# A hybrid decoder step on one core: the delta net's substitution held in a PSUM bank, and two of its state products put ahead of ScalarE's read

## The chip, the core and the metric

The kernel runs on one core of a Trainium2 chip. Five engines work side by side, each through its own queue in the order in which its instructions stand: TensorE (PE, matmuls; PEld is its weight load), VectorE (DVE), ScalarE (ACT), GpSimd (POOL) and SyncE (SP, here only an issuer of DMAs; ACT issues DMAs too, written ACTq). The metric is device time in microseconds (us) of one execution; lower is better.

## The reference

One layer of a decoder trunk over a prompt of 1024 tokens and a sample batch of 8. A combined input projection feeds three groups of heads: differential attention (the sample rows attend to 4096 cached positions each, read as pages through a page table), a Mamba-2 state-space branch, and a gated delta net. Their outputs are joined and projected back. The part that is changed is the delta net, in chunks:

```
lower = where(strict, beta * kk * decay, 0)
sol   = triangular_solve(lower + eye, rhs, lower=True, unit_diagonal=True)
u, w  = sol[..., :DV_C], sol[..., DV_C:]
def step(S, inp):
    v_new = u_c - w_c @ S
    o     = qg_c @ S + attn_c @ v_new
    S     = S * gl_c + kd_c.T @ v_new
```

## The kernel before

The program is written as Python generators, one for each stream of work, that are advanced in turn (`drive`) by weights; the recorded instructions are then put in an order by a list scheduler, which fixes each engine's queue. Three stretches follow one another. In the front, to about 875 us, the projection (`proj_fm`, line 458: each product in three matmuls of split operands) shares the engines with the pages of the sample attention, with the delta net's heads 0, 1, 2 and with smaller streams. In the middle, to about 1172 us, come the prompt's attention, the state-space scan and head 3 of the delta net. The end is the output projection (line 1831).

The pages: SP loads two pages into a tile `kt` (three buffers); GpSimd multiplies it by the queries (line 840, both operands in SBUF); VectorE sums it (line 841) into `lg`. After 16 such pairs `page_softmax` (VectorE steps on `lg`, `smx`, TensorE at lines 851, 856 and 868) makes the weights with which TensorE multiplies the values, `pv` at line 896.

A head of the delta net (`gdn_head`): the decay-weighted products go to `LT` and `AT`; the diagonal 32x32 blocks go through DRAM (`invd`) and come back as `Dm`, with four blocks of a partition's own in a row. Then 31 steps of forward substitution run on VectorE, two instructions each: `tv` = column j of the unknowns `U` times row j of `Dm`, and `U` minus `tv`. `U` is an SBUF tile of 16x32 per partition: its first half holds the unknowns, which start as an identity that GpSimd copies there (line 1138), its second half is the scratch `tv`. In the trace both are called U, so a step reads as `U<-U,Dm` and `U<-U`, at line 159 where the helper `tt` records. `gstep` remembers the newest step, and a page's multiply is ordered behind it (`behind_gdn`). After the last step ACT issues the DMAs that write U to `invd` (line 1149) and read it back into `LT`; the larger blocks are then solved by small matmuls, and `u`, `w` are formed.

The recurrence follows, eight chunks one after the other. In a chunk all four products share one PSUM bank `ps`: w by the state and the queries by the state (lines 1218, 1219), then, once VectorE has made `vn`, the state's update and the output's second part (lines 1223, 1224). ScalarE reads the queries' product into `oC` (line 155, helper `act`), VectorE makes the new state `St` and adds the second part to `oC`.

PSUM has eight banks. One is `pv`. In the front the rest are two rings: `pj` with three for the projection, and `pm` with four for everything else; `ada_gate` holds one of the four over 32 matmuls (line 1013). The first items of the projection (`LEAD` = 5) are summed side by side in two `pj` and three `pm` banks. In the middle there are other rings (`PSB`), none of which changes.

Of the kernel before, what the change touches and what calls it, by code (L numbers as in the profile page):

```python
# [9 lines left out]
F32 = mybir.dt.float32  # L10
# [3 lines left out]
AF = mybir.ActivationFunctionType  # L14
# [33 lines left out]
WB = 3  # L48
RA, RT, RB, RS, RO = "ps", "pt", "pj", "pj", "pj"
PSB = {"pj": 3, "ps": 2, "pt": 1, "pd": 1}  # L50
PSA = {"pj": 3, "pm": 4}
RG = "pj"
RW = "pd"
RD = "pd"
# [24 lines left out]
def bl(ap, n):  # L79
    return ap.unsqueeze(len(ap.shape)).broadcast_to(list(ap.shape) + [n])  # L80


def bm(ap, n):
    return ap.unsqueeze(1).broadcast_to([ap.shape[0], n] + list(ap.shape[1:]))
# [3 lines left out]
def trunk_kernel(  # L88
# [56 lines left out]
    def bank(ring=None):  # L145

        r = ring or rings[-1]
        return PS[r].tile([P, 512], F32, tag="b", name=nm("b"))
# [9 lines left out]
    def tt(out, a, b, op):  # L158
        return V.tensor_tensor(out=out, in0=a, in1=b, op=op)  # L159
# [264 lines left out]
    def proj_fm(items, ws):  # L424

        def cols(n, halo):
            h0 = halo if n else 0
            N = CH + h0 + (h0 & 1)
            return N, h0, slice((n + 1) * CH - N, (n + 1) * CH)

        ps = [bank("pj" if i < 2 else "pm") for i in range(LEAD)]
        for k in range(8):
            for i in range(LEAD):
                N, h0, sl = cols(i % 3, items[i // 3][2])
                hi, lo = ws[i // 3][k]
                for e, (a, b) in enumerate(((hi, hh), (hi, hl), (lo, hh))):
                    TE.matmul(ps[i][:, 0:N], a, b[k][:, sl], start=(k == 0 and e == 0), stop=(k == 7 and e == 2))
            if k % 2 and k < 7:
                yield 3.5 * LEAD / 4
        for i in range(LEAD):  # L440
            N, h0, sl = cols(i % 3, items[i // 3][2])
            items[i // 3][1](i % 3, ps[i][:, N - CH - h0:N])
        yield 3.5 * LEAD / 4
        ps = ws[:-1] = []
        w = ws.pop()
        for j, (c0, sink, halo) in enumerate(items):
            if 3 * j + 2 < LEAD:
                continue
            raw = w_load(items[j + 1][0], SP if j < LQ else S) if j + 1 < len(items) else []
            wn = []  # L450
            for n in range(LEAD % 3 if j == LEAD // 3 else 0, 3):
                ps = bank("pj")
                N, h0, sl = cols(n, halo)
                i = 0
                for k in range(8):
                    hi, lo = w[k]
                    for a, b in ((hi, hh), (hi, hl), (lo, hh)):
                        TE.matmul(ps[:, 0:N], a, b[k][:, sl], start=(i == 0), stop=(i == 23))  # L458
                        i += 1
                sink(n, ps[:, N - CH - h0:N])  # L460
                if n == 2:
                    for r in raw[len(wn) // 4:]:
                        wn += w_split(r)
                elif raw:
                    wn += w_split(raw[n])
                yield 3.5
            w = wn
# [572 lines left out]
    def gdn_head(h):  # L1040
# [94 lines left out]
        T64 = half([96, 8, 64], n="T64")  # L1135
        with tc.issue_after(ld.ins):
            G.memset(T64[0:32, :, 32:64], 0.0)
        G.tensor_copy(out=U[:, 0:8], in_=eye8)
        gstep.clear()
        yield W1  # L1140
        for j in range(31):
            n, m = 31 - j, j // 4 + 1
            tv = U[:, 8:16].rearrange("p a b -> p (a b)")[:, 0:m * n].rearrange("p (c i) -> p c i", i=n)
            tt(tv, bl(U[:, 0:m, j], n), bm(Dm[:, j, j + 1:32], m), ALU.mult)
            step = tt(U[:, 0:m, j + 1:32], U[:, 0:m, j + 1:32], tv, ALU.subtract)
            gstep[:] = [step.ins]
            yield 0.5
        for g in range(4):
            S.dma_start(out=invd[1, h].rearrange("b c (i g) l -> (b c) g i l", g=4)[:, g], in_=U[32 * g:32 * g + 32, 0:8])
        for b in range(4):  # L1150
# [62 lines left out]
        for c in range(8):  # L1213
            cs = slice(c * P, (c + 1) * P)
            ps = bank()
            vn = u[:, 0, :]
            if c > 0:
                TE.matmul(ps[:, 0:P], w[:, c, :], St, start=True, stop=True)
                TE.matmul(ps[:, P:256], qT[:, cs], St, start=True, stop=True)
                vn = small([P, P], "vn")  # L1220
                tt(vn, u[:, c, :], ps[:, 0:P], ALU.add)
                act(o[:, c, :], ps[:, P:256], AF.Copy, scale=f1[:, c:c + 1])
            TE.matmul(ps[:, 256:384], kN[:, c, :], vn, start=True, stop=True)
            TE.matmul(ps[:, 384:512], AT[:, c, :], vn, start=True, stop=True)
            Sn = small([P, P], "St")
            if c > 0:
                stt(Sn, St, egt[:, c, 12 + h:13 + h], ps[:, 256:384], ALU.mult, ALU.add)
                tt(o[:, c, :], o[:, c, :], ps[:, 384:512], ALU.add)
            else:
                V.tensor_copy(Sn, ps[:, 256:384])  # L1230
                S.copy(o[:, c, :], ps[:, 384:512])
            St = Sn
            yield 5.0
# [708 lines left out]
```

## Time and profile before

| | before |
|---|---|
| median of 3 runs | 1307.45 us (1305.61 to 1309.79) |
| the profiled execution | 1311.91 us, its span 1310.2 us |
| PE busy | 1145.3 us, 87% of the span |
| DVE busy | 865.4 us, 66% |
| POOL busy | 583.9 us, 45% |
| ACT busy | 470.2 us, 36% |
| HBM | 209 GB/s over the span |
| mean granted TensorE clock | 0.945 |

The span runs from the first to the last instruction. Busy time is a mean over stretches with different limits; which wait ends last has to be read in each. An engine's row shows the idle time just before it in brackets, and what ended it. [...]

### The profile page before, as it was taken

To read this page: it belongs to the slowest core of one execution; us is meant where nothing else is said; L and a number is where in the kernel's file an instruction comes from. 1 tells how busy PE (TensorE), PEld (TensorE's weight loads), DVE (VectorE), ACT (ScalarE), POOL (GpSimd) and SP (SyncE) were. 2 spreads that over 40 slices of the span, in tenths; PEclk is the share of its full clock that TensorE was granted. 3 is DMA by queue.
4 is the path that set the end of the run, shared out by engine and by line. 5 is a ranking of instruction groups with operands and counts; after the bars stand their busy time and mean duration, and the time that the engine had idled before them with its cause. 6 is when DMAs were issued, how large, how long until landed. Compare 5 with 4: busy or idle time off the path is not lost.

```text
span 1310.2 us, 21966 instructions
## 1 busy us (share of the span) xinstructions
PE 1145.3 (87%) x7364; PEld 957.1 (73%) x7365; DVE 865.4 (66%) x1994; ACT 470.2 (36%) x997; POOL 583.9 (45%) x395
## 2 busy tenths in 40 slices
PE   4999989988899678979886889888988999799997
PEld 3789987767688458759765778865656868688876
DVE  5623695398577749745656947678867888674444
ACT  6332232212213322222352142416626767552111
POOL 3757864453464634454645558453013142251100
PEclk9999999998899889989998889997889999899999
DMA  8657866984785863775779499799678473871410
GB/s 293 190 184 235 269 197 201 287 272 129 276 276 183 274 193 110 239 255 169 258 265 260 147 292 328 205 285 278 179 234 214 117 197 100 291 236 49 145 67 34
DMA packets 246449, 275.55 MB, mean 210 GB/s; under 512 B 31905, under 2 KB 163376, under 8 KB 246322
## 3 DMA queue, kind: packets, MB, share of 16 engines
q1 hardware_dynamic: 168082, 214.44, 50.9%
q10 hardware_dynamic: 78256, 59.72, 16.1%
q8 instruction: 58, 0.95, 0.3%
q14 instruction: 53, 0.43, 0.1%
HBM read 231.59 MB, written 42.67 MB: 209 GB/s over the span
## 4 chain that ended last, share of the span: by engine, by line
PE 40%; DVE 23%; DMA 19%; issue 5%; ACT 5%; POOL 4%; SPq 3%; ACTq 1%; POOLq 0%; DVEq 0%
PE b L458 15%; PE b L1831 9%; DVE U L159 5%; DMA kt<-in_cache_k_dram 4%; PE pv L896 3%; DVE cy L167 3%; DVE lg L841 3%; POOL kt L840 2%; DMA w<-in_w_in_dram 2%; DMA vt<-in_cache_v_dram 2%; DMA gs<-in_state_gdn_dram 1%; PE b L745 1%; DVE cy L969 1%; DVE e L721 1%; DMA Dm<-invd 1%
## 5 line engine op out<-in xcount | busy, mean ns | idle before, releaser
L458 PE MATMUL b<-hh,whi 128*128 128x344 f32 (+1 forms) x2016 | 505.5, 333 | 29.5 <-DVE cy L167 23.3
L840 POOL TENSOR_TENSOR kt<-kt,qb 128x1024 f32<-128x1024 f32 x128 | 305.9, 2395 | 258.4 <-DMA kt<-in_cache_k_dram 185.1
L458 PEld LDWEIGHTS b<-hh,whi 128*128 128x128 f32 x2016 | 360.9, 195 | 61.6 <-issue 32.2
L458 PE MATMUL b<-hh,wlo 128*128 128x344 f32 (+1 forms) x1008 | 330.5, 332 | 0.0
L841 DVE TENSOR_REDUCE lg<-kt 128x16 f32<-128x1024 f32 x128 | 154.8, 1213 | 145.3 <-POOL kt L840 139.7
L458 PEld LDWEIGHTS b<-hh,wlo 128*128 128x128 f32 x1008 | 195.9, 195 | 11.2 <-issue 10.1
L201 POOL TENSOR_TENSOR wlo<-w,whi 128x512 fp32r<-128x512 f32 x86 | 111.1, 1296 | 81.4 <-ACT whi L155 78.2
L1831 PE MATMUL b<-wo,mh 128*128 128x512 f32 (+1 forms) x408 | 122.2, 381 | 0.3 <-POOL wo L1565 0.3
L155 ACT ACTIVATE whi<-w 128x512 fp32r<-128x512 f32 x86 | 53.7, 630 | 151.5 <-PE b L458 111.4
L167 DVE SCALAR_TENSOR_TENSOR cy<-b,vec,cy 128x341 f32<-128x341 f32 (+4 forms) x180 | 98.5, 563 | 1.4
L896 PE MATMUL pv<-vt,wz 128*32 128x512 f32 x512 | 79.0, 647 | 16.8 <-DMA vt<-in_cache_v_dram 15.8
L1831 PEld LDWEIGHTS b<-wo,mh 128*128 128x128 f32 x408 | 74.9, 189 | 14.8 <-POOL wo L1565 0.5
L1831 PE MATMUL b<-wo,ml 128*128 128x512 f32 (+1 forms) x204 | 77.1, 378 | 0.0
L1799 POOL TENSOR_TENSOR ml<-zt,mh 128x512 fp32r<-128x512 f32 x16 | 22.4, 1405 | 102.3 <-ACT mh L1798 102.2
L159 DVE TENSOR_TENSOR U<-U,Dm 128x60 f32<-128x60 f32 (+24 forms) x124 | 53.5, 432 | 11.0 <-DMA Dm<-invd 7.1
L156 ACT ACTIVATE e<-e,nmx 128x128 f32<-128x128 f32 (+7 forms) x64 | 49.0, 767 | 9.9 <-DVE nmx L723 7.4
L155 ACT ACT_TABLE_LOAD x32 | 41.1, 1283 | 25.7 <-POOL wlo L201 11.4
L718 PE MATMUL b<-kTh,qh 128*128 128x128 f32 (+3 forms) x96 | 42.3, 443 | 8.4 <-DVE mx L721 8.2
L159 DVE TENSOR_TENSOR y<-b,gate 128x512 f32<-128x512 f32 (+1 forms) x17 | 11.1, 660 | 52.4 <-PE b L1831 52.4
L721 DVE CUSTOM_DVE_ANT_0 e<-b,bt 128x512 f32<-128x512 f32 (+3 forms) x64 | 37.0, 582 | 11.7 <-PE b L719 8.2
L1831 PEld LDWEIGHTS b<-wo,ml 128*128 128x128 f32 x204 | 38.3, 188 | 7.3
L745 PEld LDWEIGHTS b<-vh,wT 128*128 128x128 f32 x288 | 39.3, 208 | 5.8 <-ACT e L156 1.7
(531 smaller groups left out, 2015.5 us busy)
## 6 DMA issues: line engine op xcount, KB each, us to landing
kt<-in_cache_k_dram SPq DMA_DIRECT2D x256, 256.0 KB
vt<-in_cache_v_dram SPq DMA_DIRECT2D x256, 256.0 KB
w<-in_w_in_dram ACTq DMA_DIRECT2D x82, 256.0 KB
zfd<-zf ACTq DMA_DIRECT2D x12, 512.0 KB
wo<-in_w_out_dram SPq DMA_DIRECT2D x12, 512.0 KB
om<-mixd SPq DMA_DIRECT2D x24, 256.0 KB
xt<-in_x_prompt_dram SPq DMA_DIRECT2D x8, 512.0 KB
hx<-in_w_ada_dram SPq DMA_DIRECT2D x16, 256.0 KB
```

The costliest lines, as they stand in the source:

```text
L155: return S.activation(out, in_, func, bias=bias, scale=scale)
L156: return S.activation(out, in_, func, bias=bias, scale=scale, accum_out=accum)
L159: return V.tensor_tensor(out=out, in0=a, in1=b, op=op)
L167: return V.scalar_tensor_tensor(out=out, in0=a, scalar=s, in1=b, op0=op0, op1=op1)
L201: G.tensor_tensor(out=lo, in0=w32, in1=hi.bitcast(F32), op=ALU.subtract)
L458: TE.matmul(ps[:, 0:N], a, b[k][:, sl], start=(i == 0), stop=(i == 23))
L721: V.tensor_tensor_reduce(out=e[m][:, a:b], in0=ps[:, 0:b - a], in1=bias, scale=1.0, scalar=-3.0e38, op0=ALU.add, op1=ALU.max, accum_out=mx ...
L745: TE.matmul(po[:, 0:P], wTs[j // 4][:, j % 4, :], vh[:, j, :], start=(j == 0), stop=(j == i))
L840: G.tensor_tensor(out=kt, in0=kt, in1=bm(qb, 2), op=ALU.mult)
L841: V.tensor_reduce(out=lg[:, 2 * g:2 * g + 2, :], in_=kt.rearrange("p j (a d) -> p j a d", d=64), axis=AX.X, op=ALU.add)
L896: mm = TE.matmul(pv[32 * r:32 * r + 32, :], wz[:, 2 * g + j, :], vt[:, j, :], start=(b == 0 and g < 2), stop=(b == NS - 1 and g >= 14 and ...
L1831: TE.matmul(ps[c], m[a][:, kt % 4, :], w[kt][:, c[0]:c[1]], start=(kt == KT[0] and i == 0), stop=(kt == KT[-1] and i == 2))
```

## The change

The diff has two parts. First, in the front, the unknowns of the substitution move from SBUF to a PSUM bank of their own, `Up`: a new ring `pu` with one bank, taken from `pm`, which goes from four banks to three. The identity is copied there by ScalarE in place of GpSimd, the scratch `tv` stays in SBUF, and after the last step ScalarE copies the unknowns back to SBUF, from where the DMAs go out as before. One of the five lead banks of the projection is now the `pu` bank. Head 3 is solved in the middle, where there is no `pu`: its unknowns stay in SBUF, and only its identity is copied by ScalarE. Second, in the recurrence, ScalarE's read of the queries' product is recorded behind the two products of `vn` instead of ahead of them.

```diff
-PSA = {"pj": 3, "pm": 4}
+PSA = {"pj": 3, "pm": 3, "pu": 1}
...
-        ps = [bank("pj" if i < 2 else "pm") for i in range(LEAD)]
+        ps = [bank("pj" if i < 2 else "pm" if i < 4 else "pu") for i in range(LEAD)]
...
-        G.tensor_copy(out=U[:, 0:8], in_=eye8)
+        if "pu" in PS:
+            Up = PS["pu"].tile([P, 8, 64], F32, tag="b", name=nm("U"))[:, :, 0:32]
+        else:
+            Up = U[:, 0:8]
+        S.copy(Up, eye8)
...
-            tt(tv, bl(U[:, 0:m, j], n), bm(Dm[:, j, j + 1:32], m), ALU.mult)
-            step = tt(U[:, 0:m, j + 1:32], U[:, 0:m, j + 1:32], tv, ALU.subtract)
+            tt(tv, bl(Up[:, 0:m, j], n), bm(Dm[:, j, j + 1:32], m), ALU.mult)
+            step = tt(Up[:, 0:m, j + 1:32], Up[:, 0:m, j + 1:32], tv, ALU.subtract)
...
+        if "pu" in PS:
+            S.copy(U[:, 0:8], Up)
...
                 tt(vn, u[:, c, :], ps[:, 0:P], ALU.add)
-                act(o[:, c, :], ps[:, P:256], AF.Copy, scale=f1[:, c:c + 1])
             TE.matmul(ps[:, 256:384], kN[:, c, :], vn, start=True, stop=True)
             TE.matmul(ps[:, 384:512], AT[:, c, :], vn, start=True, stop=True)
             Sn = small([P, P], "St")
             if c > 0:
+                act(o[:, c, :], ps[:, P:256], AF.Copy, scale=f1[:, c:c + 1])
                 stt(Sn, St, egt[:, c, 12 + h:13 + h], ps[:, 256:384], ALU.mult, ALU.add)
```

What this makes of the queues, at three places. Line numbers behind the new lines are six higher in the kernel after. VectorE in head 0's substitution, before (a number ends each buffer's name; U_2756 is the tile of unknowns and scratch, lg the pages' sums):

```order
L841 TENSOR_REDUCE lg_1994<-kt_2901 128x16 [waits DMAHW6_49,DMAHW0_49,Pool_49]
L159 TENSOR_TENSOR U_2756<-U_2756 128x28 [waits DVE_49]
L159 TENSOR_TENSOR U_2756<-U_2756,Dm_2751 128x54 [waits DVE_49]
L159 TENSOR_TENSOR U_2756<-U_2756 128x2x27 [waits DVE_49]
L159 TENSOR_TENSOR U_2756<-U_2756,Dm_2751 128x52 [waits DVE_49]
```

and after, where U_2762 is the PSUM bank and U_2759 the SBUF tile that now holds the scratch:

```order
L159 TENSOR_TENSOR U_2759<-U_2762,Dm_2754 128x54 [waits DVE_49]
L841 TENSOR_REDUCE lg_1997<-kt_2905 128x16 [waits DMAHW1_49,Pool_49]
L159 TENSOR_TENSOR U_2762<-U_2762,U_2759 128x2x27 [waits DVE_49]
L159 TENSOR_TENSOR U_2759<-U_2762,Dm_2754 128x52 [waits DVE_49]
L159 TENSOR_TENSOR U_2762<-U_2762,U_2759 128x2x26 [waits DVE_49]
```

The steps keep their number, sizes and order, the page's sum moves by two places, and each step now has one operand in SBUF and one in PSUM. ScalarE behind the last step of head 0, before (whi is a split of the projection's weights):

```order
L155 ACT_TABLE_LOAD
L155 ACTIVATE lg_1994<-lg_1994 128x256 [waits DVE_49]
L155 ACTIVATE ses_3109<-ses_3109 128x8 [waits DVE_49]
L155 ACTIVATE whi_3628<-w_474_3512 128x512 [waits DMAHW1_49,PE_49]
L1149 DMA invd<-U_2756 256x1x32 [waits DVE_49]
```

and after:

```order
L155 ACTIVATE ses_3113<-ses_3113 128x8 [waits DVE_49]
L155 ACTIVATE whi_3633<-w_475_3517 128x512 [waits DMAHW0_49,PE_49]
L1153 COPY U_2759<-U_2762 128x256 [waits DVE_49]
L1155 DMA invd<-U_2759 256x1x32 [waits DMAHW1_49,Activation_49]
L1155 DMA invd<-U_2759 256x1x32 [waits DMAHW2_49]
```

The wait for VectorE's last step stood on the DMA and now stands on the copy, at the same place in the queue. TensorE in head 0's recurrence, chunks 1 and 2, before:

```order
L1218 MATMUL b_3851<-St_3735,kb_3331 128x128 [waits DVE_49,Activation_49]
L1219 MATMUL b_3851<-St_3735,cy_1920 128x128
L896 MATMUL pv<-vt_3668,wz 32x512 [waits DMAHW6_49,DMAHW7_49,DMAHW5_49,DMAHW0_49]
L896 MATMUL pv<-vt_3668,wz 32x512
L896 MATMUL pv<-vt_3714,wz 32x512 x2
L1223 MATMUL b_3851<-vn_3854,kN_2422 128x128 [waits Activation_49]
L1224 MATMUL b_3851<-vn_3854,AT_2521 128x128
L1218 MATMUL b_3936<-St_3859,kb_3331 128x128 [waits DVE_49]
```

and after:

```order
L1224 MATMUL b_3856<-St_3740,kb_3336 128x128 [waits DVE_49]
L1225 MATMUL b_3856<-St_3740,cy_1923 128x128
L896 MATMUL pv<-vt_3743,wz 32x512 [waits DMAHW4_49,DMAHW7_49,DMAHW3_49,DMAHW0_49]
L896 MATMUL pv<-vt_3743,wz 32x512
L896 MATMUL pv<-vt_3806,wz 32x512 x2
L1228 MATMUL b_3856<-vn_3859,kN_2425 128x128 [waits DVE_49]
L1229 MATMUL b_3856<-vn_3859,AT_2524 128x128
L1013 MATMUL b_2395<-wg_3802,cT 32x512 [waits DMAHW3_49]
L1013 MATMUL b_2395<-wg_3802,cT 32x512
L1224 MATMUL b_3941<-St_3863,kb_3336 128x128 [waits DVE_49]
```

The product of `vn` waits for VectorE in place of ScalarE; correspondingly ScalarE's read, which waited for VectorE alone, now waits for VectorE and TensorE, and VectorE's `St`, which waited for TensorE and ScalarE, waits for ScalarE alone. Elsewhere the scheduler shifts instructions by some places, most in the front and in the first half of the middle; ScalarE's queue gets three table loads more than before (52 in place of 49). The output projection keeps its order.

## Rows read from the trace of the kernel before

**Rows 1.** The page's part 4: shares of the span along the chain, by line.

```profile
PE b L458 15%; PE b L1831 9%; DVE U L159 5%; DMA kt<-in_cache_k_dram 4%; PE pv L896 3%; DVE cy L167 3%; DVE lg L841 3%; POOL kt L840 2%; DMA w<-in_w_in_dram 2%; DMA vt<-in_cache_v_dram 2%; DMA gs<-in_state_gdn_dram 1%; PE b L745 1%; DVE cy L969 1%; DVE e L721 1%; DMA Dm<-invd 1%
```

**Rows 2.** Busy time by stretch, the front from 36 us on.

```profile
36.00:875.00 839.00, 737.00 (x4842) 631.88 (x4842) 545.02 (x1029) 245.34 (x421) 466.70 (x280) 0.95 0.72 229
```

**Rows 3.** The same of tile U's VectorE instructions alone, heads 0, 1 and 2.

```profile
262.00:316.00 54.00, 31.33 (x62) 0.94 0.64 209
480.00:600.00 120.00, 19.94 (x62) 0.91 0.64 203
700.00:756.00 56.00, 28.35 (x62) 0.89 0.61 191
```

**Rows 4.** Tile U on VectorE: durations ns min/median/max, first and last start us, forms.

```profile
L159 DVE TENSOR_TENSOR U<-U,Dm x124: 153/212/2494, 264.0 to 978.5; 128x60 f32<-128x60 f32 x12, 128x28 f32<-128x28 f32 x8, 128x54 f32<-128x54 f32 x8, 128x48 f32<-128x48 f32 x8
```

**Rows 5.** The timeline in head 0's substitution: start us, us, engine, line, op, out<-in.

```profile
263.98 0.19 DVE L159 TENSOR_TENSOR U<-U,Dm 128x31 f32<-128x31 f32 x1 [1.79 <-DMA vt<-in_cache_v_dram]
...
276.82 2.38 POOL L840 TENSOR_TENSOR kt<-kt,qb 128x1024 f32<-128x1024 f32 x1
...
276.98 2.30 DVE L159 TENSOR_TENSOR U<-U 128x60 f32<-128x60 f32 x1
...
281.84 0.24 DVE L159 TENSOR_TENSOR U<-U 128x76 f32<-128x76 f32 x1
```

**Rows 6.** VectorE's vn (one PSUM operand), smx (both SBUF), as rows 4.

```profile
L159 DVE TENSOR_TENSOR vn<-vb,b x28: 266/278/289, 349.1 to 1116.4; 128x128 f32<-128x128 f32 x28
...
L159 DVE TENSOR_TENSOR smx<-smx,slfb x8: 166/710/2314, 186.6 to 928.0; 128x8 f32<-128x8 f32 x8
```

**Rows 7.** TensorE's waits, 262:325 and 695:765: us, times, longest.

```profile
PE b L851 <- DVE smx L159: 7.2, 1, 7.2
PE b L1161 <- DMA LT<-invd: 2.9, 1, 2.9
...
PE b L851 <- DVE U L159: 10.3, 1, 10.3
PE b L458 <- ACT zf L996: 4.9, 2, 3.2
```

**Rows 8.** The timeline in head 2's substitution, VectorE.

```profile
705.64 1.03 DVE L159 TENSOR_TENSOR U<-U,Dm 128x54 f32<-128x54 f32 x1
...
716.52 2.35 DVE L159 TENSOR_TENSOR U<-U,Dm 128x69 f32<-128x69 f32 x1
...
718.79 2.31 DVE L159 TENSOR_TENSOR lg<-lg,fb 128x8 f32<-128x8 f32 x1
...
722.37 2.31 DVE L159 TENSOR_TENSOR smx<-smx,slfb 128x8 f32<-128x8 f32 x1
```

**Rows 9.** Busy time by stretch, as rows 2, behind two of TensorE's waits.

```profile
725.00:735.00 10.00, 10.00 (x50) 9.76 (x50) 9.59 (x26) 0.98 (x3) 5.06 (x5) 0.77 0.11 29
...
296.00:304.00 8.00, 7.49 (x35) 6.27 (x35) 7.97 (x22) 1.01 (x1) 2.61 (x2) 0.77 0.37 102
```

**Rows 10.** Timeline, ScalarE: behind head 2's last step; a PSUM copy.

```profile
757.82 0.79 ACT L996 COPY zf<-b 128x344 f32<-128x344 f32 x2 [11.58 <-DMA invd<-U]
...
330.47 0.36 ACT L1175 COPY xs<-b 32x256 f32<-32x256 f32 x1 [0.29 <-PE b L1174]
```

**Rows 11.** The page's part 5 and groups by line: table loads, a bank's copy.

```profile
L155 ACT ACT_TABLE_LOAD x32 | 41.1, 1283 | 25.7 <-POOL wlo L201 11.4
...
L610 DVE COPY vo<-b 128x512 f32<-128x512 f32 x8 | 5.3, 686 | 2.0 <-PE b L608 2.0
```

**Rows 12.** Line 1223's wait (us, times); ScalarE's wait ahead of oC.

```profile
  ACT oC L155: 5.1, 6
...
ACT oC L155 <- DVE vn L159: 46.9, 18, 9.1
```

**Rows 13.** The bank that ada_gate holds: line 1013, as rows 4.

```profile
L1013 PE MATMUL b<-wg,cT x32: 592/592/617, 208.8 to 357.1; 128*32 128x512 f32 x32
```

**Rows 14.** The page's part 5: GpSimd's multiply of a page, and its idle time.

```profile
L840 POOL TENSOR_TENSOR kt<-kt,qb 128x1024 f32<-128x1024 f32 x128 | 305.9, 2395 | 258.4 <-DMA kt<-in_cache_k_dram 185.1
```

## The prediction

> **What bounds the kernel now.** I read the chain of work that ended last first. Its largest share is TensorE's projection, but VectorE's `U` on line 159 stands third, ahead of every load [rows 1]: a chain of tiny instructions that should be cheap. Next I read busy time by stretch. In the front TensorE is busy 737 of 839 us, VectorE 545, GpSimd 467 [rows 2]: TensorE sets the pace and loses some 102 us to waits, so a change to VectorE pays only where it ends one of these.
>
> Then `U` alone. Its 62 instructions take 31.3 us in head 0's stretch, 19.9 in head 1's and 28.4 in head 2's [rows 3], for the same sizes. The median is 212 ns and the maximum 2494 [rows 4]. The timeline shows why: a step of 31 columns takes 0.19 us and one of 76 takes 0.24, but one of 60 columns that starts at 276.98 takes 2.30 and ends at 279.28, where GpSimd's multiply of a page, begun at 276.82, ends at 279.20 [rows 5]. A step whose operands both lie in SBUF is held until the multiply is through. `smx`, with both operands in SBUF, has the same spread, 166 to 2314 ns; `vn`, with one operand in PSUM, runs between 266 and 289 in all 28 cases, although multiplies run through most of the front [rows 6].
>
> **What TensorE loses by it.** In head 0's stretch it waits 7.2 us at line 851 for `smx` and 2.9 at line 1161 for `LT`, which comes back through DRAM after the last step. In head 2's it waits 10.3 us at line 851, put down to `U`, and up to 3.2 for a projection bank that ScalarE had not read [rows 7], because ScalarE stood 11.6 us at its DMA behind the last step [rows 10].
>
> **The steps in PSUM: VectorE.** A head's 62 steps at the median are 62 x 0.212 = 13.1 us, so the hold-up is 31.3 - 13.1 = 18.2, 19.9 - 13.1 = 6.8 and 28.4 - 13.1 = 15.3 us: 40.3 us for heads 0 to 2. After the change each step has one SBUF operand, the form of `vn`, and I take the whole 40.3 as gone. Head 3 keeps its form. What a step costs in PSUM no row shows in full, since nothing on VectorE writes PSUM now. For reading there is `vn`: 128 columns in 278 ns, where the two steps above, 0.05 us for 45 columns, lead to 0.24 + 52 x 0.0011 = 0.30. So reading costs nothing extra. For writing, the bounds are 0 and a second pass over the columns, about 50 x 1.1 = 55 ns: over 186 steps 0 to 10 us of VectorE. I take 0, since `vn` is the nearest row.
>
> [...]
>
> **What of it reaches TensorE.** Head 0: VectorE is full there, 7.97 of the 8 us behind the wait [rows 9], so what it is held for moves all that is queued behind. Of the 18.2 us I put at least 7.2 ahead of `smx` and at least 7.2 + 2.9 ahead of the last step. Gain 10.1. Head 1: its 6.8 us touch no long wait; 0, at most 6.8. Head 2: not all of 10.3 goes. Of the instructions ahead of line 851 one `U` of 2.35 us and, before it, one of 1.03 are held, but so are `lg` with 2.31 and `smx` with 2.31 [rows 8], and these two keep both operands in SBUF. Gain 2.1 + 0.8 = 2.9. The last step comes earlier, and the 3.2 us behind ScalarE's DMA go with it. Together 10.1 + 2.9 + 3.2 = 16.2.
>
> [...]
>
> **ScalarE.** The identities are copied long before they are wanted, head 0's during the first projections: 0. The copy back stands between the last step and the DMA: some 0.36 us by a small copy from PSUM [rows 10], three times 1.1 us. In head 0 the 2.9 us at line 1161 are already more than covered by the 18.2, in head 2 the same holds: 0, and 1.1 if the cover is gone. Queued behind the copy, as behind the DMA before, are the splits of the weights. Three more table loads at 1.28 us [rows 11] are 3.8 us of a queue that is busy 245 of 839 [rows 2]; behind each stands a read of a projection bank or a split. I take 1, and keep 0 to 3.8.
>
> **The ring of three.** `ada_gate` holds one bank of `pm` from 208.8 to 357.1 us [rows 13], across head 0. Three others are left now, two afterwards. A product that finds no bank waits for a reading of one, 0.69 us for a full bank [rows 11]. The lead of the projection loses none, since it takes one bank less of `pm`. I take four such waits, 2.8 us, and keep 0 to 20 of them, 0 to 14 us.
>
> **The read behind the products.** Line 1223 loses 5.1 us in six cases to `oC`, and ScalarE 46.9 us waiting for `vn` ahead of it [rows 12]. After the change TensorE waits for `vn` directly. But `St`, which starts the next chunk, still needs ScalarE's read, now behind both products: vn, read, products, St becomes vn, products, read, St. The chain keeps its length; TensorE stands less and VectorE more, behind whom stand the projection's readings. I take 0, from -5 (all six waits gone) to +5.
>
> **The sum.** 16.2 + 2.5 - 1 - 2.8 = 14.9 us. What is late next are the pages: GpSimd waits 185 us in all for their loads [rows 14], and when TensorE is earlier some of lines 851 and 896 will find their pages late. The held `lg` and `smx` also stay. I let these take some 2 us: gain 13. Against its own time of 1311.9 the profiled execution would come to 1299; its time lies 4.5 us above the median of the runs, so the median comes to 1307.45 - 13 = 1294.5.
>
> **The rivals.** (1) The time goes to the next thing in line: the steps are quick, but VectorE reaches `lg` and `smx` sooner and is held there by the same multiplies, as at 718.79 and 722.37. One held instruction gets through per multiply, so head 0's gain falls to 3 or 4 of its 10, head 2's to 3, and 6.5 less the costs of 3.8 is 2.7: 1305. For it: two of the four held instructions of rows 8 stay. Against: in head 0 few of them stand between the steps. Chance 0.17. (2) Slower: the ring of three. In head 0 its own pairs of banks, the page softmax and the values' transposes share two free banks, and the queue is in order, so a wait for a bank stops the projection too. Without this term the sum is 13 + 2.8 = 15.8 us; at 0.69 us apiece it decides from 23 waits, and at 35 in the front the time is 1307.45 - 15.8 + 24.2 = 1316. For it: the bank is held for 148 us. Against: a bank's reading usually ends long before the next product. Chance 0.12. (3) Steps dearer in PSUM: at 55 ns more a step, 10 of the 40.3 us stay, a fourth of 16.2 is lost, and the time is 1298.5; 217 ns more, 40.3 / 186, would cancel the gain, and no row comes near. [...] Chance 0.07. (4) It doesn't do what it says: a step with one PSUM operand is held all the same; then only costs are left, 1307.45 + 3.8 = 1311. `vn` speaks against it. Chance 0.03.
>
> **How the numbers follow.** The forecast has 0.61: 1294.5, between 1280 (all bounds kind: 16.2, head 1's 6.8 and the read's 5, without costs) and 1303. A measurement of this kernel tells about 0.3%, 4 us, from no change: faster is below 1303.5, slower above 1311.4. Faster: 0.61 and 0.07, less 0.03 for weak cases of both, and 0.03 of rival 1: 0.68. Same: 0.14 of rival 1, 0.03 and half of rival 4, 0.02: 0.19. Slower: 0.12 and the rest of rival 4: 0.13. The range runs from 1280 to 1310 and leaves out rival 2 and a little at the low end.
>
> **What would show it.** Right: the steps of heads 0 to 2 have a maximum near 0.3 us and some 13 us a head; TensorE's waits of 7.2 and 2.9 in head 0 are gone and that of 10.3 is near 7; ScalarE's wait behind head 2's last step is short; line 1223 waits for `vn`. Wrong: steps of 2 us remain; line 608, 851 or the small solves wait for a reading of another tile; `St` waits long for ScalarE; or the long waits return at the next held instruction, with the front as long as before. The forecast fails as a whole if the shifted queues cost more than 13 us somewhere far from the heads, which these rows cannot show.

## The result, and the profile after

The kernel after takes 1323.84 us (median of 4 runs, 1316.92 to 1331.12), the kernel before 1308.22: a ratio of 1.0111, interval 1.0072 to 1.0151. It is slower by some 15 us, outside the forecast range, although what the change was read to do on VectorE took place. The profiled execution of after took 1323.39 us, its span is 1321.7.

First the substitution. A line by stretch reads start:end and length, then the busy us (and instructions) of each engine in the order PE, PEld, DVE, ACT, POOL (or of the one that was asked for), the granted share of TensorE's clock, the DMA engines' busy share and GB/s. The tile U on VectorE in the kernel after, as [rows 3] (busy time in three stretches, one per head) and [rows 4] (durations in ns, min/median/max); `U<-U,Dm` are the products, of which those of heads 0 to 2 read PSUM, `U<-U,U` are the steps that write PSUM, `U<-U` is head 3, which stays in SBUF. The last line is the kernel before, where all steps that write U are `U<-U`:

```profile
240.00:330.00 90.00, 13.09 (x62) 0.98 0.82 251
430.00:620.00 190.00, 12.76 (x62) 0.91 0.66 210
690.00:770.00 80.00, 12.93 (x62) 0.86 0.75 222
...
L159 DVE TENSOR_TENSOR U<-U,Dm x124: 154/207/458, 274.5 to 974.7; 128x60 f32<-128x60 f32 x12, 128x28 f32<-128x28 f32 x8, 128x54 f32<-128x54 f32 x8, 128x48 f32<-128x48 f32 x8
L159 DVE TENSOR_TENSOR U<-U,U x93: 172/217/360, 274.7 to 752.4; 128x60 f32<-128x60 f32 x9, 128x28 f32<-128x28 f32 x6, 128x54 f32<-128x54 f32 x6, 128x48 f32<-128x48 f32 x6
L159 DVE TENSOR_TENSOR U<-U x31: 174/207/1144, 935.2 to 974.9; 128x60 f32<-128x60 f32 x3, 128x28 f32<-128x28 f32 x2, 128x54 f32<-128x54 f32 x2, 128x48 f32<-128x48 f32 x2
...
L159 DVE TENSOR_TENSOR U<-U x124: 158/210/2405, 264.2 to 978.7; 128x60 f32<-128x60 f32 x12, 128x28 f32<-128x28 f32 x8, 128x54 f32<-128x54 f32 x8, 128x48 f32<-128x48 f32 x8
```

The three heads take 38.8 us together where [rows 3] have 79.6; the medians are within 7 ns of those before, and the steps of over 2 us are gone. In the timeline of head 0 a step of 0.21 us now runs inside GpSimd's multiply, which in [rows 5] held one for 2.30:

```profile
280.37 2.40 POOL L840 TENSOR_TENSOR kt<-kt,qb 128x1024 f32<-128x1024 f32 x1 [2.18 <-DVE U L159]
280.62 0.21 DVE L159 TENSOR_TENSOR U<-U,Dm 128x50 f32<-128x50 f32 x1
280.86 0.22 DVE L159 TENSOR_TENSOR U<-U,U 128x50 f32<-128x50 f32 x1
```

TensorE's waits over the front (36:875), where [rows 7] had 7.2 and 10.3 us at line 851; and the busy times of the front, as [rows 2]:

```profile
PE b L458 <- DVE cy L167: 15.1, 3, 11.2
PE pv L896 <- DMA vt<-in_cache_v_dram: 13.9, 5, 5.3
...
PE b L1228 <- DVE vn L159: 7.5, 5, 2.6
...
PE b L851 <- DVE smx L159: 1.9, 1, 1.9
...
36.00:875.00 839.00, 741.56 (x4889) 629.03 (x4882) 512.26 (x1034) 253.92 (x431) 464.45 (x276) 0.94 0.73 229
```

The waits at line 851 have shrunk to 1.9 us, VectorE is busy 33 us less in the front, and TensorE 4.6 us more, so it has done more by then. So the front is no longer than before, and yet the kernel is. To find the place I set the start of the same matmul (the n-th of a line, counted from the first matmul of the program) in each trace against the kernel before. The first column is that matmul's time in the kernel before, from the span's start. A plus is later than before, in us; each column is one profiled execution, within 5 us of its kernel's median but for the unknowns in their own bank, 7 us faster than its median:

```
before's time  place                 after   banks alone   unknowns in own bank   own bank, transposes on four   ring of four
  86 us        projection             +5.6      +8.2           +10.0                  +1.4                           -0.8
 206           projection            +10.7     +18.8           +16.3                  +2.3                           -0.6
 299           behind head 0          +3.5     +17.5            +8.8                  -7.4                           -8.2
 561           projection             -5.9     +10.4            -5.4                 -12.1                          -20.5
 872           end of the front       -4.0     +15.1            -2.0                  -6.9                          -25.2
 981           sample's state         -2.0     +13.6            -8.3                  -9.1                          -25.2
1033           prompt's attention    +11.0     +15.3            -8.3                  -9.0                          -15.2
1149           output projection     +12.8     +13.6            -7.5                  -7.9                          -12.3
```

The columns to the right of after are experiments told below. After loses up to 10.7 us in the first 206, before any substitution; wins it back over the heads; and loses some 13 between 981 and 1033, far from any edit of the front.

**The start.** Busy time by stretch, before (the first two lines) and after:

```profile
36.00:60.00 24.00, 22.89 (x225) 18.77 (x226) 14.25 (x38) 8.61 (x20) 17.76 (x19) 1.00 0.71 203
60.00:92.00 32.00, 30.54 (x191) 29.72 (x190) 10.78 (x49) 12.58 (x24) 16.98 (x13) 1.00 0.48 169
...
36.00:60.00 24.00, 21.70 (x254) 17.82 (x247) 11.41 (x31) 7.42 (x18) 12.95 (x14) 0.93 0.69 196
60.00:92.00 32.00, 29.81 (x178) 28.02 (x177) 14.47 (x54) 12.06 (x24) 19.83 (x16) 0.98 0.45 147
```

Three of TensorE's waits in 24:92 of the kernel after, which have no counterpart of that size before, where line 437 waits 0.2 us:

```profile
PE b L437 <- ACT hh L417: 2.0, 1, 2.0
PE b L383 <- ACT hx L386: 0.8, 1, 0.8
PE b L398 <- DVE hx L388: 0.8, 1, 0.8
```

Line 383 transposes the input into banks of `pm`, which ScalarE and VectorE read; the last two waits are for such readings. They are short, and the last transpose starts no later than before (32.0 us, before 32.3). The longest wait is that of the lead (line 437) for its operands `hh`, which ScalarE makes of `hx` once VectorE has scaled it (line 415). VectorE's queue at that place, before (the first two lines) and after:

```profile
49.61 1.91 DVE L415 TENSOR_SCALAR hx<-hx,modT 128x512 f32<-128x512 f32 x4
52.46 0.87 DVE L1639 TENSOR_SCALAR pt<-pt 1x256 int32<-1x256 int32 x1 [0.94 <-DMA pt<-in_page_table_dram]
...
51.66 0.28 DVE L1645 TENSOR_SCALAR pt<-pt 1x256 int32<-1x256 int32 x1 [2.56 <-DMA pt<-in_page_table_dram]
...
53.92 0.23 DVE L1670 TENSOR_SCALAR rb<-rb 4x32 f32<-4x32 f32 x1 [0.72 <-DMA rb<-in_rel_bias_dram]
...
54.15 1.90 DVE L415 TENSOR_SCALAR hx<-hx,modT 128x512 f32<-128x512 f32 x4
```

The kernel before scales this part of `hx` ahead of small steps on the page table (`pt`) and the relative bias (`rb`), which wait for loads from DRAM. With three banks the scheduler's order puts the scaling behind them, and it starts 4.5 us later. The lead waits for it, the granted clock over 36 to 60 us is 0.93 in place of 1.00, and the lead's last matmul is 4.3 us later (74.3, before 70.0). So the smaller ring acts here through the order, and hardly through waits for a bank. From 86 to 206 us another 5 are lost, in waits of which none is longer than 2.6.

**The middle.** Busy time by stretch, before (first three lines) and after:

```profile
995.00:1005.00 10.00, 8.07 (x51) 6.52 (x50) 6.74 (x12) 6.34 (x16) 5.63 (x5) 1.00 0.89 247
1005.00:1015.00 10.00, 8.71 (x78) 7.46 (x77) 8.59 (x28) 6.51 (x19) 1.27 (x1) 0.83 0.50 135
1015.00:1025.00 10.00, 9.21 (x121) 8.17 (x120) 7.28 (x24) 9.87 (x31) 2.60 (x2) 1.00 0.33 97
...
995.00:1005.00 10.00, 7.44 (x33) 4.45 (x33) 5.62 (x20) 6.11 (x14) 3.93 (x3) 0.73 1.08 298
1005.00:1015.00 10.00, 8.56 (x32) 4.41 (x29) 4.99 (x11) 3.30 (x5) 0.00 (x0) 0.76 0.53 136
1015.00:1025.00 10.00, 7.88 (x60) 6.83 (x61) 8.14 (x12) 4.17 (x13) 3.60 (x2) 0.58 0.37 115
```

TensorE is busy 24 us of the 30 in place of 26, but on 125 matmuls in place of 250, at a granted clock of 0.58 to 0.76. SyncE's queue in the kernel after (DMA issues), then ScalarE's:

```profile
987.76 0.38 SPq L531 DMA_DIRECT2D mixd<-oA  x1
991.16 1.98 SPq L1342 DMA_DIRECT2D mixd<-yv  x1
993.38 4.26 SPq L823 DMA_DIRECT2D vt<-in_cache_v_dram  x2
998.79 10.62 SPq L1565 DMA_DIRECT2D wo<-in_w_out_dram  x2
...
1011.03 0.57 ACT L943 COPY oS<-b 8x512 f32<-8x512 f32 x1 [5.35 <-PE b L941]
1013.58 1.15 ACT L155 ACTIVATE wo<-wo,vec 128x1024 fp32r<-128x1024 f32 x1 [1.32 <-DMA wo<-in_w_out_dram]
1014.64 0.58 ACT L155 ACTIVATE ems<-b 128x512 f32<-128x512 f32 x1
```

and the same instructions before:

```profile
981.95 1.25 SPq L823 DMA_DIRECT2D vt<-in_cache_v_dram  x2
...
991.60 0.37 SPq L531 DMA_DIRECT2D mixd<-oA  x1
...
998.21 0.57 ACT L943 COPY oS<-b 8x512 f32<-8x512 f32 x1 [4.29 <-PE b L745]
998.70 0.58 ACT L155 ACTIVATE ems<-b 128x512 f32<-128x512 f32 x1
```

The last value pages of the sample are issued 11 us later, behind two stores; so the sample's result `oS` is read at 1011 instead of 998, and the state-space scan's `ems`, which stood right behind it, now stands behind a scaling of `wo` too, which waits for its load. `ems` comes 16 us later.

### The profile page after: what moved, and what is told of

Read it like the earlier page. It is cut to its first block, busy times and chain, and to the rows that moved or that the text cites. A ratio compares the mean times of both kernels' runs of the same rounds, so it can differ in the third digit from the quotient of the medians.

```text
span 1321.7 us, 21959 instructions
## 1 busy us (share of the span) xinstructions
PE 1155.2 (87%) x7362; PEld 961.0 (73%) x7365; DVE 830.2 (63%) x1994; ACT 477.8 (36%) x1007; POOL 580.9 (44%) x391
## 4 chain that ended last, share of the span: by engine, by line
PE 49%; DMA 22%; DVE 13%; issue 5%; POOL 4%; ACT 4%; SPq 3%; ACTq 1%; POOLq 0%; DVEq 0%
PE b L458 18%; PE b L1837 10%; DMA kt<-in_cache_k_dram 5%; PE pv L896 4%; DMA vt<-in_cache_v_dram 3%; DMA w<-in_w_in_dram 2%; PE b L745 2%; DVE cy L167 2%; POOL kt L840 2%; DVE lg L841 2%; DMA gs<-in_state_gdn_dram 2%; DMA kTh<-kfd 1%; POOL wlo L201 1%; PE b L718 1%; SPq L823 1%
## 5 line engine op out<-in xcount | busy, mean ns | idle before, releaser
L458 PE MATMUL b<-hh,whi 128*128 128x344 f32 (+1 forms) x2016 | 498.0, 330 | 21.4 <-DVE cy L167 15.1
L458 PEld LDWEIGHTS b<-hh,whi 128*128 128x128 f32 x2016 | 356.0, 193 | 52.7 <-issue 26.2
L201 POOL TENSOR_TENSOR wlo<-w,whi 128x512 fp32r<-128x512 f32 x86 | 110.9, 1297 | 111.2 <-ACT whi L155 99.3
L896 PE MATMUL pv<-vt,wz 128*32 128x512 f32 x512 | 85.5, 670 | 37.4 <-DMA vt<-in_cache_v_dram 18.2
L896 PEld LDWEIGHTS pv<-vt,wz 128*32 128x32 f32 x512 | 12.2, 113 | 51.3 <-issue 33.6
L745 PE MATMUL b<-vh,wT 128*128 128x128 f32 x288 | 44.6, 306 | 1.2 <-ACT oA L155 0.9
L745 PEld LDWEIGHTS b<-vh,wT 128*128 128x128 f32 x288 | 40.8, 217 | 6.7 <-ACT wT L738 1.8
```

Source lines behind the costliest of these rows:

```text
L201: G.tensor_tensor(out=lo, in0=w32, in1=hi.bitcast(F32), op=ALU.subtract)
L745: TE.matmul(po[:, 0:P], wTs[j // 4][:, j % 4, :], vh[:, j, :], start=(j == 0), stop=(j == i))
L896: mm = TE.matmul(pv[32 * r:32 * r + 32, :], wz[:, 2 * g + j, :], vt[:, j, :], start=(b == 0 and g < 2), stop=(b == NS - 1 and g >= 14 and ...
```

## The experiments

Two theories were set against each other from the first experiments on. B: the bank that is taken from `pm` costs more than the quick steps gain. M and later O: the loss comes from the order that the scheduler makes of the whole program. Rivals of both: the moved read (R), head 3's identity on ScalarE (H). Medians in us, ratio to the kernel before on the same chip with its interval:

| run | median | ratio |
|---|---|---|
| e1 unknowns in their own bank, read as before | 1312.05 | 1.0027 (0.9993 to 1.0061) |
| e2 moved read alone | 1306.47 | 0.9966 (0.9926 to 1.0005) |
| e3 banks alone | 1326.27 | 1.0143 (1.0089 to 1.0196) |
| e4 after, head 3's identity on GpSimd | 1324.23 | 1.0103 (1.0048 to 1.0158) |
| e5 unknowns in a bank of the ring of four | 1299.90 | 0.9915 (0.9883 to 0.9948) |
| e6 e5 and the moved read | 1298.49 | 0.9927 (0.9898 to 0.9957) |
| e7 e1, transposes on four banks | 1305.04 | 0.9975 (0.9948 to 1.0002) |
| e8 after, last values ahead | 1319.88 | 1.0085 (1.0055 to 1.0114) |
| e9 before, weight 2.5 | 1337.96 | 1.0228 (1.0184 to 1.0273) |
| e10 e1, weight 2.5 | 1341.42 | 1.0243 (1.0197 to 1.0288) |
| e11 e5, weight 2.5 | 1320.21 | 1.0105 (1.0063 to 1.0147) |
| e12 e6, last values ahead | 1289.32 | 0.9858 (0.9800 to 0.9917) |
| e13 after, weight 2.5 | 1346.05 | 1.0278 (1.0227 to 1.0329) |
| e14 identities on ScalarE alone | 1311.90 | 1.0015 (0.9981 to 1.0049) |
| e15 before, weight 2.6 | 1324.61 | 1.0133 (1.0093 to 1.0174) |
| e16 e1, weight 2.6 | 1349.39 | 1.0315 (1.0278 to 1.0351) |
| e17 e5, weight 2.6 | 1313.05 | 1.0053 (1.0021 to 1.0086) |

**The change taken apart (e1 to e4, e14).** e1 is after with the read of `ps` put back ahead of the products; e2 is before with nothing but that read moved behind them; e3 is before with the ring and the lead's banks of the diff's first two hunks alone. e4 and e14:

```diff
# e4: after, with
-        S.copy(Up, eye8)
+        if "pu" in PS:
+            S.copy(Up, eye8)
+        else:
+            G.tensor_copy(out=Up, in_=eye8)
# e14: before, with
-        G.tensor_copy(out=U[:, 0:8], in_=eye8)
+        S.copy(U[:, 0:8], eye8)
```

> The first part alone: the unknowns in PSUM with the ring of three, ScalarE's read of the queries' product left where it was in the kernel before. In the profile of the kernel after, TensorE ends the front some 5 us earlier than before and stands 11.7 us later from about 1016 us on, so some 17 us are lost in the middle, around the end of head 3's solve. Theory M (order of the middle): the loss comes from how the scheduler puts the loads and ScalarE's instructions in line there. This kernel's SP queue stands there much nearer to before's; if the loss is gone with it, 1298 to 1306 us, front as early as in the kernel after. Theory R (the moved read costs it): 1298 to 1306 as well, and the kernel with the read alone slow. Theory B (the bank taken away costs it): 1316 to 1326, and the kernel with the banks alone slow too.

> The second part alone: the kernel before with ScalarE's read of the queries' product behind the two products. Theory R: this carries the loss in the middle, 1318 to 1326 us. Theories M and B: the read itself is worth nothing, 1304 to 1312 us; line 1223 then waits for vn and no longer for oC.

> The ring alone: three banks of pm, the fourth set apart and used only as the fifth lead bank; the unknowns in SBUF with the identity copied by GpSimd, the read at its old place. Theory B: it loses what the kernel after loses and has no gain, 1320 to 1332 us; the profile shows some 5 us lost in the first 70 us and waits for a reading of a bank in the front. Theory M: the lost bank costs 3 to 8 us at the start and the rest depends on the order in the middle, 1309 to 1318 us. The steps stay held up, U up to 2.4 us.

> The kernel after with the identity of head 3 copied by GpSimd as before, so that ScalarE's queue is one copy shorter in the middle; TensorE's and VectorE's queues stand exactly as in the kernel after. Theory H (ScalarE's copy of head 3's identity delays the solve and with it the middle): 1304 to 1311 us. Theories M, R and B: as the kernel after, 1318 to 1328 us.

> The kernel before with nothing but the four identities copied by ScalarE in place of GpSimd; TensorE's and VectorE's queues stand exactly as in the kernel before. The prediction put this at nothing: 1304 to 1312 us. Rival: ScalarE's copies, which wait for a buffer of the tile, hold up the splits and reads behind them, 1313 us or more.

The banks alone cost 1326.27 - 1308.74 = 17.5 us. The unknowns in that bank win 14.2 of them back (e3 to e1), the moved read then adds 11.8 (e1 to after), and the three steps make up after's 15. H is out: e4 is as slow as after, and e14 shows no difference from before. R in its simple form is out: alone, the read is worth -2 us, not told from nothing. B's range held for e3. e1 fell between the ranges: that it was not at 1298 to 1306 speaks against M as the only cause, and B, which had 1316 to 1326, had not reckoned with what the unknowns win. Each of these steps also changes the scheduler's order, whose own price is told below, so their sizes hold for this order. The jump in the middle is no accident of one execution: e4, whose TensorE and VectorE queues are those of after, stands at -0.2 at 872 and at +9.5 at 1033.

**The bank given back (e5 to e7).** e5 and e6 take the bank of the unknowns from `pm`, which keeps four; e7 lets the transposes use the bank that stands apart:

```diff
# e5 (read as before) and e6 (read moved)
-PSA = {"pj": 3, "pm": 3, "pu": 1}
+PSA = {"pj": 3, "pm": 4}
...
-        if "pu" in PS:
-            Up = PS["pu"].tile([P, 8, 64], F32, tag="b", name=nm("U"))[:, :, 0:32]
+        if "pm" in PS:
+            Up = PS["pm"].tile([P, 8, 64], F32, tag="b", name=nm("U"))[:, :, 0:32]
# e7: e1 with, in the transposes of the input,
-            pst = bank()
+            pst = bank("pu" if k % 4 == 3 else "pm")
```

> The unknowns in PSUM without a bank set apart: the ring pm keeps its four banks, the unknowns of a head take one of them for the time of their steps, the lead is as before; the read stays at its old place. Theory B, as the runs so far shape it: the unknowns in PSUM are worth some 14 us (1326.3 for the banks alone, 1312.0 with the unknowns in the bank), and the bank missing from pm costs some 17 us, 8 to 10 of it already by 70 us, where the transposes of the input run through three banks. Then this kernel loses nothing before 200 us and comes to 1291 to 1299 us. Rival O: the bank is not what costs, every order of the scheduler comes out some 10 us apart by chance; then 1304 to 1318 us, and the first 200 us may lose as well.

> As the run before, and with ScalarE's read behind the two products. Alone the read was worth -2 us (interval -10 to +1). Theory B: 1288 to 1299 us, the middle without the jump that the kernel after shows. Rival R2: the read costs 12 us whenever the unknowns are in PSUM, as between the first part alone (1312) and the kernel after (1324): 1303 to 1312 us.

> The unknowns in a bank of their own and the read at its old place, but the transposes of the input at the start may use that bank too, every fourth of them, so that they run through four banks as before. Theory B: the 5 us by 65 us and with them the lower clock behind are gone, some 8 us; what the ring of three costs between 120 and 200 us stays: 1301 to 1307 us. Rival: the start was late for another reason, and the time stays at 1309 to 1316 us.

In the timeline of e5 the identities are copied at 241, 454 and 664 us and copied back at 307, 516 and 731: a head holds its bank for 62 to 67 us, and the rest of the front has four. With the bank taken only for that time the change is a gain, 0.9915 (0.9 us above B's range) and 0.9927, and R2 is out here: the read adds nothing. e7 wins 7 us on e1, and the table of places says where: +10.0 and +16.3 at 86 and 206 become +1.4 and +2.3. So what is lost in the first 206 us comes and goes with the transposes' fourth bank; that much of B is shown. The way is again VectorE's queue: in e7 the scaling of `hx` stands ahead of `pt` and starts at 46.7. The same holds in every trace of this study, those in the other orders below included. In the eight whose transposes have three banks (after, e1, e3, e4, e8, e10, e13, e16) it stands behind `pt` and starts at 53.4 to 54.5, the lead's last matmul is 4 to 6 us later than before, and 11 to 19 us are lost by 206. In the ten others and before it starts at 46.7 to 49.6, and these ten stand at -1 to +1 and at -4 to +3. No run moved these steps of VectorE alone. e7 still ends 5 us behind e5 and its front 18. A part of that is seen in e7's head 1, VectorE and then TensorE:

```profile
476.71 0.19 DVE L159 TENSOR_TENSOR U<-U,Dm 128x31 f32<-128x31 f32 x1 [7.04 <-DMA Dm<-invd]
...
477.44 0.94 PE L458 MATMUL b<-hh,whi 128*128 128x344 f32 x2 [10.26 <-DVE cy L167]
```

The first step of the head, which waits for `Dm` from DRAM, stands ahead of three of VectorE's readings of a projection bank; VectorE waits 7.0 us, and TensorE 10.3 for the bank. The kernel before has such a wait as well, with VectorE at 4.0; in e5 the longest wait of line 458 for `cy` is 1.4. Whether the bank or only the order made this difference, these runs don't tell.

**The order as such (e8 to e13, e15 to e17).** One weight was moved, by which the streams of pages are advanced; not one instruction differs, only the order:

```diff
# e9, e10, e11, e13 (2.5) and e15, e16, e17 (2.6)
-                    yield 2.4
+                    yield 2.5
```

> A control for the order alone: the kernel before with one weight of the generators moved, by which the page streams are advanced (2.4 to 2.5 a pair of key pages); no instruction, size or buffer differs, only the order in which the scheduler puts them. It asks how much of any difference here is the order. Theory O (orders come out some 10 us apart by chance): 1300 to 1320 us, more than 6 us off 1309 as likely as not. Theory B (the bank and the unknowns decide, the order adds little): 1304 to 1314 us.

> The same weight moved in the first part alone (unknowns in a bank of their own, pm with three; 1312 us with the old weight). Theory B: again slower than the ring of four by 8 to 16 us with this weight, about 1308 to 1316 us. Theory O: anywhere from 1298 to 1322 us, above or below the ring of four.

> The same weight moved in the kernel with the unknowns in a bank of the ring of four (1299.9 us with the old weight). Theory B: some 9 us below the kernel before with this weight, 1295 to 1304 us. Theory O: no steady distance, 1293 to 1315 us.

> The kernel after with the page weight moved from 2.4 to 2.5. With this weight the first part alone came to 1341 us, so the distance is what the moved read adds in another order. With the old weight it was +12 us (1312 to 1324), without the own bank -2 and -1. Theory O (the +12 are an accident of the order in the middle): 1328 to 1344 us, at or below the first part alone. Theory R2 (the read costs 12 us with a bank of its own): 1349 to 1357 us.

> The kernel before with the page weight at 2.6, the third order of the same instructions (2.4: 1309, 2.5: 1338). Theory O: anywhere between 1300 and 1345 us.

> The first part alone (own bank) with the weight at 2.6. In the two orders so far it lay 3 and 4 us above the kernel before with the same weight and 12 and 21 us above the ring of four. Theory B: again within 8 us of the kernel before with this weight, and 10 us or more above the ring of four. Theory O: any sign.

> The unknowns in a bank of the ring of four with the weight at 2.6. In the two orders so far it lay 9 and 18 us below the kernel before with the same weight. Theory B: 8 to 20 us below it again. Theory O: any sign.

The order alone moves the kernel before by 29 and 18 us, more than the whole result; both expectations for e9 were too narrow, and so were the times that e10 and e11 were put at. For one weight the distances hold their sign: ring of four less before is -9, -18 and -12 us; own bank less ring of four +12, +21 and +36; own bank less before +3, +3 and +25, of which only the last is clear of the intervals. At the end of the front (872 us) the own bank's traces stand 23, 18 and 23 us behind the ring of four's. So B holds over three orders, with a size that hangs on the order. What the read adds beside the own bank falls from 11.8 us to 4.6 (e10 to e13, intervals overlapping), between the ranges of both theories: this points to the one order for most of the 11.8, and doesn't show it. e16 lies 25 us above e15, which theory B had put at under 8: the own bank can cost more than it cost here.

Where the moved weight costs its time is one place too. In all seven of these traces 19 to 31 us are lost between 1033 and 1149, against -2 to +10 in the others, while e9 and e15 end the front 8 and 29 us earlier than before. In these seven the last product with the sample's value pages starts at 1017 to 1113 us, in all others at 968 to 1005. No run moved these pages alone in the new orders, so that they are the cause there is argued.

The middle was then touched alone:

```diff
# e8 (in after; g >= 14) and e12 (in e6; g >= 8)
-        for j in range(2):
-            page(cache_v, b * NPG + 2 * g + j, vt[:, j, :])
+        with boost(2000 if b == NS - 1 and g >= 8 else 0):
+            for j in range(2):
+                page(cache_v, b * NPG + 2 * g + j, vt[:, j, :])
```

> The kernel after, with the loads of the last two pairs of value pages of the last sample row put earlier in SP's queue, ahead of a store of the state-space branch that waits there; up to about 960 us all queues stand exactly as in the kernel after. In the kernel after TensorE loses some 13 us between 985 and 1025 us: SP reaches the last values at 993 and 997 us behind the stores, ScalarE's copy of the sample's result waits for it until 1011, and the state-space step's copy stands behind that copy. Theory M: with the loads earlier 5 to 13 us come back, 1310 to 1319 us. Rival: the wait is only one of several with the same end, and the time stays at 1321 to 1327 us.

> The ring of four with the read moved (1298.5 us), and the value pages of the last sample row put ahead in SP's queue: four of them now stand ahead of the second of the sample's state loads gs, where they stood behind it one by one; up to some 900 us all queues are the same. In the ring of four TensorE leaves the front some 25 us earlier than before, and of that 10 are given back between 960 and 1010 us, where the last eight page pairs take 35 us instead of 23. Theory M: SP's order of gs and the last values takes part of it, 1290 to 1296 us. Rival: something else ends last there, 1297 to 1302 us.

e8 lies 4 us below after, not told apart by these runs, and wins less than was expected; at 1033 its matmuls stand at -0.9 against after's +11.0, at 1149 at +7.8. Most of the jump is gone at its place, and most of what was won there is lost again behind it. In e12 the same kind of edit wins 9 us on e6 (the intervals overlap a little) and makes the fastest kernel of the study, 20.6 us below the kernel before and just below M's range. What it moves is seen in the last products with the value pages (first and last start us) and in SP's queue, e6 first, then e12:

```profile
L896 PE MATMUL pv<-vt,wz x64: 589/617/1062, 915.2 to 971.8; 128*32 128x512 f32 x64
...
946.87 0.33 SPq L823 DMA_DIRECT2D vt<-in_cache_v_dram  x1
949.77 0.39 SPq L1499 DMA_DIRECT2D gs<-in_state_gdn_dram  x1
950.35 0.44 SPq L823 DMA_DIRECT2D vt<-in_cache_v_dram  x1
953.62 0.39 SPq L1533 DMA_DIRECT2D gs<-in_state_gdn_dram  x1
...
957.09 4.10 SPq L823 DMA_DIRECT2D vt<-in_cache_v_dram  x3
```

```profile
L897 PE MATMUL pv<-vt,wz x64: 589/617/1063, 918.9 to 968.0; 128*32 128x512 f32 x64
...
950.99 2.45 SPq L823 DMA_DIRECT2D vt<-in_cache_v_dram  x4
953.85 0.39 SPq L1500 DMA_DIRECT2D gs<-in_state_gdn_dram  x1
956.59 0.39 SPq L1534 DMA_DIRECT2D gs<-in_state_gdn_dram  x1
958.62 0.97 SPq L823 DMA_DIRECT2D vt<-in_cache_v_dram  x2
```

In e6 pages and state loads alternate, and the queue stands still for 2.6 and 2.8 us ahead of the state loads at 949.77 and 953.62; in e12 four pages go ahead, and the last product starts 3.8 us earlier. Against before, e6 stands at -31.3, -24.3 and -17.3 at 981, 1033 and 1149, e12 at -28.3, -27.7 and -22.4: e6 loses 7.0 us between the first two, e12 0.6. It is the place where the ring of four without the read (e5) gave back 10 of its 25 us of front (table of places, 981 to 1033).

## Why the prediction was wrong

**Right: the steps.** 40.3 us of hold-up were to go; 79.6 - 38.8 = 40.8 went. The price of a step in PSUM was put at 0 to 55 ns with 0 taken; the medians are 207 and 217 ns for 212 and 210, which held steps raise a little. Rivals 3 and 4 fall. `smx` stays held, 149/814/2323 ns, as the prediction said.

**Right: what reaches TensorE, in size.** 16.2 us were read off the waits at lines 851, 1161 and 458. No run shows the 2.5 that the sum adds for the clock: over 296:304 and 725:735 the granted clock of after is 1.00, where [rows 9] have 0.77 twice, but over the whole front it is 0.94, where [rows 2] have 0.95. The unknowns in PSUM are worth 14.2 in time where nothing else of the banks changes (e3 to e1), and 9 to 18 in the ring of four over three orders; in the front of its trace 25. Part of how near this comes is luck, since e3 and e1 differ in their order as well, and the order alone is worth as much.

**Right: ScalarE's copies.** They cost nothing that e14 or e4 shows; table loads in the part of the page that lists them went from 32 to 35.

**Wrong: the ring of three.** This is the step that failed: "I take four such waits, 2.8 us", and before it "The lead of the projection loses none, since it takes one bank less of `pm`". The banks alone cost 17.5. The lead does have its five banks, but it starts late, and the sentence missed what runs ahead of it: the transposes of the input on the same ring. The prediction priced the ring by waits for a bank's reading, from line 1013's bank on, 208.8 to 357.1 [rows 13]; the loss was there by 206, and what the runs showed in place of such waits is VectorE's queue, in which the scaling of the lead's operands went behind waits for loads, 4.5 us, as in every trace with three banks for the transposes. Rival 2 named the right resource and side (1316), but by waits for banks in head 0, not by late operands at the start; its chance of 0.12 was too low.

**Wrong: the shifted queues.** The prediction's last condition came true, twice: queues that moved far from the heads cost 10.7 us by 206, as above, and 13 more between 981 and 1033. These were put at nothing in the sum. For the read it took 0, from -5 to +5; alone and in the ring of four this holds (-2, -1), and line 1228 waits for `vn` as said, but the kernel with the own bank and the read lies 11.8 above the own bank alone, and its trace puts 13 into the middle's order. "What is late next" was put at 2 us for the pages; in the ring of four the front's 25 us shrink to 12 in the middle, 10 of them about the last pages of the sample, and e12, which moves these, lies 9 below e6.

**Open.** How the own bank's remaining cost between 299 and 872 us splits into bank and order, and why e16 is so much slower than e15: of the 19 us between their traces 9 are there by 206 and 17 by 872, so most is lost in the front.

## What to carry to other kernels

A buffer that is held for three times 65 us of 870 should come from a ring that others use the rest of the time, not out of it: the same steps in PSUM won nothing with a bank set apart (e1) and 1% in a shared ring (e5). When a ring shrinks, list every user of it from the program's first instruction, not only those near the edit, and compare the queues of the engines that feed them: here no bank was waited for long, but a scaling went behind waits for loads. Where a scheduler orders the whole program, price the order itself with a variant that moves nothing but the order, and then look for the one late load; here that was worth as much as the edit.

## What was not expected of the hardware

A step with one operand in PSUM and its result in PSUM took as long as one in SBUF (217 against 210 ns in the median) and ran through GpSimd's multiplies unheld, 360 ns at most over 93 steps, where two SBUF operands had been held up to 2.5 us. Separate runs of the kernel before spread by 12 to 27 us on a chip (11 to 25 runs; 1297 to 1324 at the widest), so a single profiled execution places a loss but doesn't size it below some 10 us; e14's was 12 us below its own median.
